# Six blocks of 512 columns in the first stage of a decoder trunk, four of them summed in SBUF from quarter pieces

## The chip, the core and the metric

The kernel runs on one core of a Trainium2 chip. The metric is the device time of one execution in microseconds (us), the median over executions. TensorE (PE in the profile) multiplies matrices, VectorE (DVE) and ScalarE (ACT) do elementwise work, SyncE (SP) issues nearly all DMAs, GpSimd (POOL) only eight small ones.

## The reference

A two-layer decoder trunk on 256 tokens of width 2048, all in float32. Layer 0 mixes with native sparse attention, layer 1 with stick-breaking attention; each is followed by a SwiGLU channel mixer. A vector c, one per sequence, gives each layer a shift, a scale and a gate (adaLN). What concerns the change is the start of layer 0:

```python
c_act = silu(c)
mod = c_act @ mod_w[0] + mod_b[0]                 # 2048 x 12288 weights
sh1, sc1, g1, sh2, sc2, g2 = split(mod, 6)
h = rms_norm(x, norm_g[0, 0]) * (1 + sc1) + sh1   # 256 x 2048
proj = h @ a_w_in                                 # 2048 x 5168
q, kc, vc, ks, vs, kw, vw, g = split(proj, ...)   # q: 2048 columns, six of 512, g: 48
q, kc, ks, kw = rope(...)                         # kc, vc: then compressed by an MLP (cmp_w1, cmp_w2)
o = gates[0]*attend(q, kc', vc') + gates[1]*attend(q, ks, vs) + gates[2]*attend(q, kw, vw)
x = x + g1 * rms_norm(o @ a_w_out, norm_g[0, 1])
```

## The kernel before, in words

Everything is read once from HBM, 657 MB. A weight comes in pieces of 512 rows by 512 columns, 1 MB each (`raw`). ACT rounds a piece to fp32r (`wh`), DVE takes the rest (`wl`), and TensorE multiplies three times for each 128 rows: `hh*wh`, `hh*wl`, `hl*wh`, where `hh` and `hl` are the same two parts of the activations (one page `hA` for each quarter of the 2048 rows). A piece is so 4 x 3 = 12 matmuls of 512 columns for each of the two token tiles t, 24 in all. A block of 512 output columns needs four such pieces, one for each quarter of the rows; its two accumulators (`acc`, one for each t) are two of the eight PSUM banks.

The shift and the scale of layer 0 must be known before the first `hA`. They are computed in quarters of 512 columns: eight loads of 1 MB (`modq`, four row quarters of two vectors), each used by four matmuls with a 32-column result (`qacc`); ACT copies the sum (`qrow`), TensorE transposes it (`pmq`), DVE adds it up (`mall`), and ACT and DVE make `hA` from it. The other vectors (`modw` loads, 16 for each vector) are multiplied and summed by DVE (`macc`, one instruction for each load); when a vector's sum is complete, four matmuls (`pmod`) add it up over the partitions (`mod_fin`).

The first stage before takes three blocks (kc, vc, ks) quarter by quarter: all three are held in six banks from quarter 0 to quarter 3. Then come kw, the first compression weights (`rawd`, which are not split), vs, the second ones, vw, the gates (`gacc`), four blocks of q, and under those the attention of 16 heads (`cs`, `sc`, `oT`), then the output projection (`wh,oA`) and the channel mixer.

The order on every engine is written out ahead by a planner (class `Emit`), which walks through the units of TensorE's work and gives each instruction a start and an end by a table of costs (`_cost`). It decides when a loaded piece is split, when a `macc` step is taken, and which work of the epilogues (generators, `spawn`) comes between the matmuls. On the chip each engine takes its instructions strictly in the order that the planner wrote. Buffers: 21 pages of 128 x 2048 (weights, `hA`, loads, sums), eight half-size `s2` buffers, eight banks. At most RAW_AHEAD = 7 loads are outstanding ahead of their splitting; SP issues them in the order of the list `order`, which is made at the end of the program. `when_free` and `get` keep MM_BANKS banks for accumulators.

Of the kernel before, what the change touches and what calls it, by code (L numbers as in the profile page):

```python
# [39 lines left out]
N_BANKS = 8  # L40
MM_BANKS = 3
RAW_AHEAD = 7
SPLIT_AHEAD = 2
# [3 lines left out]
LAGR = 1  # L47
K_LATE = 1
TAIL = 6
TAIL0 = 6  # L50
HEAD = 2
HEAD0 = 0
T1_LEAD = 2.0
# [83 lines left out]
class Emit:  # L137
# [4 lines left out]
    def __init__(self, nc):  # L142
# [16 lines left out]
        self.ahead = 0  # L159
        self.target = SPLIT_AHEAD  # L160
        self.reserve = SPLIT_AHEAD
        self.wait_pages = 0
# [64 lines left out]
    def when_free(self, tag):  # L227

        f = self.free[BANKS.get(tag, tag)]
        keep = max(0, MM_BANKS - self.mm) if tag == "x" else 0  # L230
        return f[0] if len(f) > keep else None

    def get(self, tag, name, *a, keep=0):
# [3 lines left out]
        while True:  # L237
            f = self.free[BANKS.get(tag, tag)]
            low = len(f) <= keep + (max(0, MM_BANKS - self.mm) if tag == "x" else 0)
# [166 lines left out]
def kernel(ctx: ExitStack, tc, consts, x, c, mod_w, mod_b, norm_g, ffn_w_in, ffn_w_out, a_w_in,  # L406
# [108 lines left out]
    def mac_load(vec, k):  # L515
# [6 lines left out]
        def mac(sl):  # L522
# [329 lines left out]

    def rope_T(acc, t, dst, tag="mm"):

# [8 lines left out]
        V.tensor_tensor(v1, av, cosT[:, t].unsqueeze(1).to_broadcast([P, 4, DH]), op=OP.mult)  # L863
        E.put(tag)
        V.tensor_tensor(t1, t1, t2, op=OP.add)
# [31 lines left out]

    def ep_k(acc, t, name, i, tag):
        dst = yield from get_kv(name)
        yield from rope_T(acc, t, dst[:, i], tag=tag)  # L900
        E.flag((name, i, t))
# [5 lines left out]

    def ep_v(acc, t, i):
        dst = yield from get_kv("v")
        copy(dst.rearrange("p s g n -> p s (g n)").rearrange("p s (t n) -> p s t n", t=2)[:, i, t], acc)  # L910
        E.put("mm")
        E.flag(("v", i, t))

    gates = {}
# [39 lines left out]

    def ep_q(acc, t, g):
        dst = yield from get_q("A", g)
        yield from rope_T(acc, t, dst)
        E.flag(("q", g, t))
# [301 lines left out]
    def emit_lag(us, lag):  # L1260
# [3 lines left out]
        while j < len(us):  # L1264
# [10 lines left out]
    col = {"q": 0, "kc": 2048, "vc": 2560, "ks": 3072, "vs": 3584, "kw": 4096, "vw": 4608, "g": 5120}  # L1275
    ko = [mm_units("kc", w0, col["kc"], 0, range(4), "hA", lambda a, t, nb: ep_k(a, t, "kvc", 0, "mm")),
          mm_units("vc", w0, col["vc"], 0, range(4), "hA", lambda a, t, nb: ep_vc(a, t)),
          mm_units("ks", w0, col["ks"], 0, range(4), "hA", lambda a, t, nb: ep_k(a, t, "ksw", 0, "mm"))]
    for kt in range(KT):
        for blk in ko:  # L1280
            units.extend(blk[kt])
    n_ko = len(units)
    emit_plain(mm_units("kw", w0, col["kw"], 0, range(4), "hA", lambda a, t, nb: ep_k(a, t, "ksw", 1, "mm")))
    for i in range(4):
        units.append(dict(kind="cmp", key=("w1", 0, i), s=0, i=i))
    emit_plain(mm_units("vs", w0, col["vs"], 0, range(4), "hA", lambda a, t, nb: ep_v(a, t, 0)))
    for i in range(4):
        units.append(dict(kind="cmp", key=("w1", 1, i), s=1, i=i))
    emit_plain(mm_units("vw", w0, col["vw"], 0, range(4), "hA", lambda a, t, nb: ep_v(a, t, 1)))
    units.append(dict(kind="gate", key=("wg",)))  # L1290
    for g in range(4):
        emit_plain(mm_units("q", w0, col["q"] + g * NB, g, range(4), "hA", lambda a, t, nb: ep_q(a, t, nb)))

# [260 lines left out]
```

## Time and profile before

| | us |
|---|---|
| median of three runs (2491.67 to 2493.23) | 2492.37 |
| profiled execution, time | 2491.2 |
| its span, first to last instruction | 2489.4 |
| PE busy | 2381.8 |
| DVE busy | 1584.3 |
| ACT busy | 1072.8 |

What lies outside the span is 1.8 us. The page gives PE as busy for 96% of the span and as 90% of the chain of work that ended last. Matmuls overlap, so a PE that is busy by the page isn't one at its peak: one matmul of 512 columns has a duration of 0.39 us, while the next one starts 0.23 us after it. An idle PE, or one at a lower granted clock, is what the rows below show.

### The profile page before, as it was taken

To read this page: it belongs to the slowest core of one execution; us is meant where nothing else is said; L and a number is where in the kernel's file an instruction comes from. 1 tells how busy PE (TensorE), PEld (TensorE's weight loads), DVE (VectorE), ACT (ScalarE), POOL (GpSimd) and SP (SyncE) were. 2 spreads that over 40 slices of the span, in tenths; PEclk is the share of its full clock that TensorE was granted. 3 is DMA by queue.
4 is the path that set the end of the run, shared out by engine and by line. 5 is a ranking of instruction groups with operands and counts; after the bars stand their busy time and mean duration, and the time that the engine had idled before them with its cause. 6 is when DMAs were issued, how large, how long until landed. Compare 5 with 4: busy or idle time off the path is not lost.

```text
span 2489.4 us, 26996 instructions
## 1 busy us (share of the span) xinstructions
PE 2381.8 (96%) x11086; PEld 1916.5 (77%) x11086; DVE 1584.3 (64%) x1275; ACT 1072.8 (43%) x1195; POOL 4.5 (0%) x12
## 2 busy tenths in 40 slices
PE   5789999998999999999998999999899999999998
PEld 2467777787888787878877887888788888888787
DVE  2357878968777666767767777775655544554554
ACT  3232355455333334333445455665533334434442
POOL 0000000000000000000000000000000000000000
PEclk9899999999999999999999999999999999999999
DMA  9979956767988779877757979776565646865642
GB/s 353 386 268 375 364 185 220 269 239 281 343 296 296 267 269 373 323 271 286 288 200 273 381 245 354 254 282 224 203 221 201 203 169 215 309 203 190 215 170 102
DMA packets 261532, 657.54 MB, mean 264 GB/s; under 512 B 12448, under 2 KB 21920, under 8 KB 236064
## 3 DMA queue, kind: packets, MB, share of 16 engines
q1 hardware_dynamic: 260704, 651.59, 72.9%
q0 software_dynamic: 704, 4.23, 0.4%
q8 instruction: 87, 1.43, 0.2%
q14 instruction: 37, 0.30, 0.0%
HBM read 653.64 MB, written 2.13 MB: 263 GB/s over the span
## 4 chain that ended last, share of the span: by engine, by line
PE 90%; DVE 4%; ACT 4%; issue 1%; DMA 0%; SPq 0%; DVEq 0%; ACTq 0%
PE acc L109 82%; DVE wl L109 1%; ACT wh L109 1%; PE z L109 1%; PE qacc L109 1%; PE sc L109 1%; PE oT L109 1%; DVE macc L109 1%; PE aT L109 1%; PE pmod L109 1%; ACT hf L109 1%; PE hid L109 1%; PE hT L109 1%; DMA modq<-in_mod_w_dram 0%; SPq L109 0%
## 5 line engine op out<-in xcount | busy, mean ns | idle before, releaser
L109 DVE TENSOR_TENSOR wl<-raw,wh 128x2048 fp32r<-128x2048 f32 x385 | 878.5, 2287 | 569.5 <-ACT wh L109 512.5
L109 ACT ACTIVATE wh<-raw 128x2048 fp32r<-128x2048 f32 x385 | 732.3, 1910 | 632.6 <-PE acc L109 452.0
L109 PE MATMUL acc<-wh,hhF 128*128 128x512 f32 x2816 | 882.2, 391 | 1.2 <-ACT hhF L109 1.1
L109 PEld LDWEIGHTS acc<-wh,hhF 128*128 128x128 f32 x2816 | 529.3, 188 | 115.6 <-issue 2.5
L109 PE MATMUL acc<-wl,hhF 128*128 128x512 f32 x1408 | 548.8, 390 | 1.1 <-DVE wl L109 1.1
L109 PE MATMUL acc<-wh,fa 128*128 128x512 f32 x1408 | 436.6, 390 | 0.0
L109 DVE SCALAR_TENSOR_TENSOR macc<-modw,cact,macc 128x2048 f32<-128x2048 f32 x180 | 422.3, 2346 | 11.4 <-DMA modw<-in_mod_w_dram 8.6
L109 PEld LDWEIGHTS acc<-wl,hhF 128*128 128x128 f32 x1408 | 264.8, 188 | 55.5 <-DVE wl L109 1.9
L109 PEld LDWEIGHTS acc<-wh,fa 128*128 128x128 f32 x1408 | 264.3, 188 | 55.4 <-issue 0.8
L109 PE MATMUL acc<-wl,fa 128*128 128x512 f32 x704 | 273.9, 389 | 0.0
L109 PE MATMUL acc<-wh,hA 128*128 128x512 f32 x640 | 226.0, 413 | 19.0 <-ACT wh L109 19.0
L109 PEld LDWEIGHTS acc<-wh,hA 128*128 128x128 f32 x640 | 123.8, 193 | 67.1 <-issue 22.3
L109 PE MATMUL acc<-wh,hhK 128*128 128x512 f32 x512 | 164.5, 398 | 3.0 <-ACT hhK L109 2.6
L109 PEld LDWEIGHTS acc<-wl,fa 128*128 128x128 f32 x704 | 132.2, 188 | 27.2
L109 PE MATMUL acc<-wl,hA 128*128 128x512 f32 x320 | 128.7, 402 | 8.7 <-DVE wl L109 8.7
L109 PEld LDWEIGHTS acc<-wh,hhK 128*128 128x128 f32 x512 | 97.3, 190 | 24.8 <-ACT hhK L109 2.8
L109 PE MATMUL acc<-wl,hhK 128*128 128x512 f32 x256 | 100.8, 394 | 3.2 <-DVE wl L109 3.2
L109 ACT ACTIVATE fa<-aT 128x512 fp32r<-128x512 f32 x43 | 25.6, 595 | 175.3 <-PE aT L109 160.5
L109 PE MATMUL acc<-wh,hhB 128*128 128x512 f32 x256 | 86.7, 404 | 1.8 <-ACT wh L109 1.8
L109 PE MATMUL acc<-wh,oA 128*128 128x512 f32 x256 | 83.0, 396 | 0.0
L109 PE MATMUL acc<-wh,oB 128*128 128x512 f32 x256 | 82.1, 394 | 0.0
L109 PEld LDWEIGHTS acc<-wl,hA 128*128 128x128 f32 x320 | 62.1, 194 | 21.3 <-DVE wl L109 11.2
(175 smaller groups left out, 1619.5 us busy)
## 6 DMA issues: line engine op xcount, KB each, us to landing
raw<-in_ffn_w_in_dram SPq DMA_DIRECT2D x176, 1024.0 KB, 5.5
modw<-in_mod_w_dram SPq DMA_DIRECT2D x160, 1024.0 KB, 7.1
raw<-in_ffn_w_out_dram SPq DMA_DIRECT2D x88, 1024.0 KB, 5.2
raw<-in_a_w_in_dram SPq DMA_DIRECT2D x40, 1024.0 KB, 10.1
modq<-in_mod_w_dram SPq DMA_DIRECT2D x32, 1024.0 KB, 14.3
modw<-in_kv_mod_w_dram SPq DMA_DIRECT2D x32, 1024.0 KB, 5.1
raw<-in_kv_w_dram SPq DMA_DIRECT2D x32, 1024.0 KB, 8.7
raw<-in_a_w_out_dram SPq DMA_DIRECT2D x16, 1024.0 KB, 5.7
```

Of the source, the lines that this page charges most:

```text
L109: return f(*a, **k)
```

## The change

1. The first stage takes six blocks in each quarter: kc and vc accumulate in four banks as before; ks, kw, vs and vw are computed in pieces of one quarter (`ep_piece`): each piece has a bank of its own for 12 matmuls. The first quarter is copied to a `part` page by ACT, the next ones are added to it by DVE, and at the last quarter rope works from `part` (ks, kw) or the sum is written to `v` (vs, vw).
2. In the first stage six banks are kept for accumulators (MM_START), afterwards three as before.
3. The list of loads: all eight `modq` of quarter 0, then the six weights of a quarter with the eight `modq` of the next quarter between them, and in the first three quarters one `modw` behind them. The first vector's four `modq` come before the second's.
4. After the first stage: the first block of q, the first compression weights, the gates, the second ones, and the other three blocks of q. Five keys (HEAD0) are passed before further `modw` are spread.
5. The planner's costs for matmuls, DMA and some DVE forms are others, and `mod_fin` starts 2.0 us later in the plan.

```diff
-K_LATE = 1
+MM_START = 6
+EARLY_Q = 0
-HEAD0 = 0
+HEAD0 = 5
+EXTRA_AT = (5,)
...
         if op == "transpose":
-            return 0.107
-        if out.shape[0] <= 64 and ins[1].dtype == F32 and n >= 256:
-            return n * 4 / 2400.0 * (0.25 if out.shape[0] <= 32 else 0.5)
-        return max(n * (4 if ins[1].dtype == F32 else 1) / 2400.0, 0.104)
+            return 0.109
+        if ins[1].dtype != F32:
+            return max(n / 2400.0 + 0.0133, 0.04)
+        if out.shape[0] <= 64 and n >= 256:
+            return n / 2400.0 + 0.09 if out.shape[0] <= 32 else n * 2 / 2400.0 + 0.02
+        return 2 * max(n * 2 / 2400.0 + 0.0133, 0.109)
...
     if eng == "DMA":
-        return n * 4 * P / 360e3 + 0.05
+        return n * 4 * P / 383e3
...
-    return 0.07 + n / (1920.0 if fast else 960.0)
+    ptr = 0.055 * (op in ("tensor_scalar", "scalar_tensor_tensor"))
+    return 0.075 + ptr + n / (1920.0 if fast else 960.0)
...
-        keep = max(0, MM_BANKS - self.mm) if tag == "x" else 0
+        keep = max(0, self.mm_banks - self.mm) if tag == "x" else 0
...
-                    E.spawn(mod_fin(vec))
+                    E.spawn(after(mod_fin(vec), E.fin + 2.0))
...
+    def ep_piece(acc, t, place, p, final):
+
+        if p:
+            yield from E.wait(("part", place, t, p - 1))
+        s = yield from part_of(place, t)
+        if p == KT - 1 and final[0] == "v":
+            yield from ep_v(acc, t, final[1], s, lambda: part_done(place))
+            return
+        if p == 0:
+            A.activation(s, acc, AF.Copy)
+        else:
+            V.tensor_tensor(s, acc, s, op=OP.add)
+        E.put("mm")
+        E.flag(("part", place, t, p))
+        if p == KT - 1:
+            yield
+            if final[0] == "q":
+                yield from ep_q(s, t, final[1], lambda: part_done(place))
+            else:
+                yield from ep_k(s, t, "ksw", final[1], lambda: part_done(place))
...
+    early = [("ks", 0, (0, 0), ("k", 0)), ("kw", 0, (0, 1), ("k", 1)), ("vs", 0, (1, 0), ("v", 0)),
+             ("vw", 0, (1, 1), ("v", 1))] + [("q", g, (2, g), ("q", g)) for g in range(EARLY_Q)]
     for kt in range(KT):
-        for blk in ko:
+        for blk in whole:
             units.extend(blk[kt])
+        for seg, nb, place, final in early:
+            emit_plain(mm_units(seg, w0, col[seg] + nb * NB, nb, [kt], "hA",
+                                lambda a, t, nb_, place=place, final=final, kt=kt: ep_piece(a, t, place, kt, final)))
     n_ko = len(units)
...
+    call(lambda: setattr(E, "mm_banks", MM_BANKS))
+    late = [mm_units("q", w0, col["q"] + g * NB, g, range(4), "hA", lambda a, t, nb: ep_q(a, t, nb))
+            for g in range(EARLY_Q, 4)]
+    emit_plain(late[0])
+    for s in range(2):
+        for i in range(4):
+            units.append(dict(kind="cmp", key=("w1", s, i), s=s, i=i))
+        if s == 0:
+            units.append(dict(kind="gate", key=("wg",)))
+    for blk in late[1:]:
+        emit_plain(blk)
...
     k0 = keys_of(0, n_ko)
+    qs = [[("modq", (0, i), q, kt) for i in (1, 0) for kt in range(KT)] for q in range(KT)]
+    order += qs[0]
+    m0 = mods_of([(0, 2), (0, 4), (0, 3)])
+    per = len(k0) // KT
     for q in range(KT):
-        order += [("modq", (0, i), q, kt) for i, kt in ((1, 0), (0, 2), (1, 1), (0, 3), (0, 0), (1, 2), (0, 1), (1, 3))]
-        order += k0[max(0, q * 3 - K_LATE):q * 3 + 3 - K_LATE]
-    order += k0[len(k0) - K_LATE:]
-    order += spread(keys_of(n_ko, n_l0), mods_of([(0, 2), (0, 4), (0, 3)]), TAIL0, HEAD0)
+        ws, ms = k0[q * per:(q + 1) * per], qs[q + 1] if q + 1 < KT else []
+        for i, w in enumerate(ws):
+            order.append(w)
+            order += ms[i * len(ms) // per:(i + 1) * len(ms) // per]
+            if q < KT - 1 and i in EXTRA_AT:
+                order.append(m0.pop(0))
+    order += spread(keys_of(n_ko, n_l0), m0, TAIL0, HEAD0)
```

TensorE executes the same number of instructions; DVE gets 19 more and ACT 10 more.

The order on TensorE at the end of a quarter, before (`hA_79` is the page of the second quarter of rows, and `wh_110` ends that quarter):

```order
L109 MATMUL acc_70_378<-wl_90_465,hA_79_434 128x512
L109 MATMUL acc_70_378<-wh_89_464,hA_79_434 128x512
L109 MATMUL qacc_95_499<-modq_91_468,cact_116 32x512 x4
L109 MATMUL pmq_103_583<-K_67,qrow_102_581 128x128 x4
L109 MATMUL qacc_93_483<-modq_94_488,cact_116 32x512 x4
L109 MATMUL pmq_106_598<-K_67,qrow_105_596 128x128 x4
L109 MATMUL acc_88_457<-wh_110_617,hA_79_434 128x512
L109 MATMUL acc_88_457<-wl_111_618,hA_79_434 128x512
L109 MATMUL acc_88_457<-wh_110_617,hA_79_434 128x512 x2
L109 MATMUL acc_88_457<-wl_111_618,hA_79_434 128x512
```

The last `modq` and both transposes stand behind all matmuls whose weights are split; TensorE goes on with `wh_110`, the quarter's last piece, which stands on ACT behind the next `hA`.

The same place in the change (`hA_52` is the page of quarter 0, `pmq_96` the last transposes of the next quarter's vectors):

```order
L111 MATMUL acc_93_499<-wh_81_432,hA_52_290 128x512
L111 MATMUL qacc_79_419<-modq_72_385,cact_116 32x512 x4
L111 MATMUL acc_93_499<-wh_81_432,hA_52_290 128x512
L111 MATMUL acc_93_499<-wl_82_433,hA_52_290 128x512
L111 MATMUL acc_93_499<-wh_81_432,hA_52_290 128x512
L111 MATMUL pmq_96_515<-K_67,qrow_95_513 128x128 x4
L111 MATMUL acc_93_499<-wh_81_432,hA_52_290 128x512
L111 MATMUL acc_93_499<-wl_82_433,hA_52_290 128x512
L111 MATMUL acc_93_499<-wh_81_432,hA_52_290 128x512 x2
```

Behind `pmq_96` stand 42 matmuls of quarter 0 and one `modq` until the first matmul with `hA_97`, the page of quarter 1.

DVE in the second quarter of the change (`part` are the sums, `wl` the split weights, `mall` and `hA` the next quarter's activations):

```order
L111 TENSOR_TENSOR wl_125_696<-raw_106_562,wh_124_695 128x2048
L111 TENSOR_TENSOR part_85_442<-acc_127_701,part_85_442 128x512
L111 TENSOR_TENSOR wl_131_735<-raw_113_603,wh_130_734 128x2048
L111 TENSOR_TENSOR part_85_442<-acc_128_714,part_85_442 128x512
L111 TENSOR_TENSOR part_85_442<-acc_133_740,part_85_442 128x512
L111 TENSOR_REDUCE mall_118<-pmq_138_779 128x4
L111 TENSOR_TENSOR mall_118<-mall_118,vecT_109 128x4
L111 TENSOR_SCALAR hf_140_790<-xnT_21_156,mall_118 128x256
L111 CAST hA_139_789<-hf_140_790 128x512
L111 TENSOR_TENSOR hA_139_789<-hf_140_790,hA_139_789 128x512
L111 TENSOR_TENSOR hA_139_789<-hf_141_795,hA_139_789 128x512
L111 TENSOR_TENSOR wl_143_801<-raw_115_637,wh_142_800 128x2048
```

The additions to `part` stand between the splits of the next weights, and `wl_143`, the quarter's last piece, stands behind the next quarter's `hA_139`.

TensorE at one of the partition sums (`pmod`) in layer 0's channel mixer, before and then in the change:

```order
L109 MATMUL acc_872_5448<-wl_864_5395,hhF0_630_3752 128x512
L109 MATMUL acc_872_5448<-wh_863_5394,hhF0_630_3752 128x512
L109 MATMUL pmod_874_5464<-macc_768_4676,K_67 32x512 x4
L109 MATMUL acc_869_5431<-wh_867_5427,hhF0_635_3778 128x512
L109 MATMUL acc_869_5431<-wl_868_5428,hhF0_635_3778 128x512
L109 MATMUL acc_869_5431<-wh_867_5427,hhF0_635_3778 128x512
```

```order
L111 MATMUL acc_898_5502<-wh_894_5483,hhF0_660_3824 128x512
L111 MATMUL acc_898_5502<-wl_895_5484,hhF0_660_3824 128x512
L111 MATMUL acc_898_5502<-wh_894_5483,hhF0_660_3824 128x512
L111 MATMUL pmod_903_5539<-macc_787_4666,K_67 32x512 x4
L111 MATMUL acc_898_5502<-wh_894_5483,hhF0_660_3824 128x512
L111 MATMUL acc_898_5502<-wl_895_5484,hhF0_660_3824 128x512
```

In the plan `pmod` may stand no earlier than 2.0 us after its sum's end, where it stood as soon as the sum was there; here it moves into a unit that has begun.

## Rows read from the trace of the kernel before

**Rows 1.** The page: busy time, share of the span and instructions of each engine.

```profile
PE 2381.8 (96%) x11086; PEld 1916.5 (77%) x11086; DVE 1584.3 (64%) x1275; ACT 1072.8 (43%) x1195; POOL 4.5 (0%) x12
```

**Rows 2.** Who waited for whom, TensorE, 39 to 152 us: total, times, longest.

```profile
PE acc L109 <- ACT wh L109: 19.0, 4, 4.8
...
PE pmq L109 <- ACT qrow L109: 4.3, 6, 0.7
```

**Rows 3.** TensorE in order of time at a quarter's end: start, duration, instruction, idle before.

```profile
105.41 1.06 PE L109 MATMUL qacc<-modq,cact 128*32 128x512 f32 x8
107.19 0.66 PE L109 MATMUL pmq<-K,qrow 128*128 128x128 f32 x4 [0.72 <-ACT qrow L109]
112.58 0.80 PE L109 MATMUL acc<-wh,hA 128*128 128x512 f32 x1 [4.74 <-ACT wh L109]
114.91 0.80 PE L109 MATMUL acc<-wl,hA 128*128 128x512 f32 x1 [1.53 <-DVE wl L109]
115.50 1.05 PE L109 MATMUL acc<-wh,hA 128*128 128x512 f32 x2
116.36 0.63 PE L109 MATMUL acc<-wl,hA 128*128 128x512 f32 x1
```

**Rows 4.** Windows of that end: length, busy by engine, clock, DMA share, GB/s.

```profile
107.85:112.58 4.73, 0.00 (x0) 0.00 (x0) 2.74 (x8) 4.06 (x6) 0.00 (x0) 0.92 1.05 388
112.58:120.74 8.16, 6.62 (x19) 4.67 (x19) 6.68 (x3) 3.55 (x2) 0.00 (x0) 0.63 1.05 387
83.47:107.85 24.38, 22.94 (x127) 11.75 (x126) 0.34 (x2) 1.19 (x2) 0.00 (x0) 1.00 1.04 386
```

**Rows 5.** TensorE in order of time within that quarter.

```profile
93.93 1.06 PE L109 MATMUL qacc<-modq,cact 128*32 128x512 f32 x8
94.93 0.50 PE L109 MATMUL acc<-wh,hA 128*128 128x512 f32 x1
95.26 0.39 PE L109 MATMUL acc<-wl,hA 128*128 128x512 f32 x1
95.49 0.62 PE L109 MATMUL acc<-wh,hA 128*128 128x512 f32 x2
95.96 0.40 PE L109 MATMUL acc<-wl,hA 128*128 128x512 f32 x1
```

**Rows 6.** Groups by line: busy, mean ns of one, idle before.

```profile
L109 DVE TENSOR_TENSOR wl<-raw,wh 128x2048 fp32r<-128x2048 f32 x385 | 878.5, 2287 | 569.5 <-ACT wh L109 512.5 <-PE acc L109 41.6 <-DMA raw<-in_ffn_w_in_dram 8.6
L109 ACT ACTIVATE wh<-raw 128x2048 fp32r<-128x2048 f32 x385 | 732.3, 1910 | 632.6 <-PE acc L109 452.0 <-DVE wl L109 87.2 <-DVE macc L109 38.1
...
L109 DVE SCALAR_TENSOR_TENSOR macc<-modw,cact,macc 128x2048 f32<-128x2048 f32 x180 | 422.3, 2346 | 11.4 <-DMA modw<-in_mod_w_dram 8.6 <-DMA modw<-in_kv_mod_w_dram 2.4
...
L109 DVE TENSOR_TENSOR yp<-acc,yp 128x512 f32<-128x512 f32 x16 | 11.0, 687 | 24.4 <-PE acc L109 24.4
...
L109 ACT ACTIVATE yp<-acc 128x512 f32<-128x512 f32 x16 | 9.4, 590 | 13.1 <-DVE wl L109 6.6 <-PE acc L109 6.5
...
L109 PE MATMUL hid<-rawd,xpe 128*64 128x256 f32 x128 | 14.7, 384 | 0.0
```

**Rows 7.** Windows of the stages behind the first one.

```profile
190.00:300.00 110.00, 102.94 (x554) 83.89 (x553) 81.10 (x56) 34.36 (x28) 0.00 (x0) 0.98 1.03 387
300.00:550.00 250.00, 242.54 (x1246) 189.01 (x1245) 202.44 (x329) 135.09 (x282) 1.16 (x2) 0.99 0.65 228
```

**Rows 8.** The same view, instructions on macc alone.

```profile
150.00:300.00 150.00, 1.93 (x8) 0.20 (x8) 51.73 (x23) 0.97 0.91 339
300.00:550.00 250.00, 2.13 (x16) 0.34 (x16) 57.58 (x25) 0.99 0.65 228
```

**Rows 9.** Who waited for whom, TensorE, the whole span.

```profile
PE pmod L109 <- DVE macc L109: 12.0, 7, 3.1
```

**Rows 10.** The same view, 152 to 560 us.

```profile
PE acc L109 <- DVE wl L109: 4.1, 2, 2.6
...
PE cs L109 <- DVE pc L109: 2.9, 1, 2.9
```

**Rows 11.** TensorE in order of time, the first weight piece.

```profile
44.03 0.80 PE L109 MATMUL acc<-wh,hA 128*128 128x512 f32 x1 [4.80 <-ACT wh L109]
```

More of the change, by code (lines that the diff above doesn't have):

```diff
@@ L160, in __init__ @@
         self.target = SPLIT_AHEAD
+        self.mm_banks = MM_START
         self.reserve = SPLIT_AHEAD
@@ L238, in get @@
             f = self.free[BANKS.get(tag, tag)]
-            low = len(f) <= keep + (max(0, MM_BANKS - self.mm) if tag == "x" else 0)
+            low = len(f) <= keep + (max(0, self.mm_banks - self.mm) if tag == "x" else 0)
             if not low and f[0] <= self.now + 0.2:
@@ L851, with put_mm, rope_T @@
     qT = {}
-    def rope_T(acc, t, dst, tag="mm"):
+    def put_mm():
+        E.put("mm")
+    def rope_T(acc, t, dst, done):
         av = acc.rearrange("p (h d) -> p h d", h=4)
@@ L863, in rope_T @@
         V.tensor_tensor(v1, av, cosT[:, t].unsqueeze(1).to_broadcast([P, 4, DH]), op=OP.mult)
-        E.put(tag)
+        done()
         V.tensor_tensor(t1, t1, t2, op=OP.add)
@@ L896, in plain_T, with ep_k @@
         yield from T_out(s, t, dst)
-    def ep_k(acc, t, name, i, tag):
+    def ep_k(acc, t, name, i, done=put_mm):
         dst = yield from get_kv(name)
-        yield from rope_T(acc, t, dst[:, i], tag=tag)
+        yield from rope_T(acc, t, dst[:, i], done)
         E.flag((name, i, t))
@@ L906, in ep_vc, with ep_v, part_of, part_done @@
         E.flag(("kvc", 1, t))
-    def ep_v(acc, t, i):
+    def ep_v(acc, t, i, part, done):
         dst = yield from get_kv("v")
-        copy(dst.rearrange("p s g n -> p s (g n)").rearrange("p s (t n) -> p s t n", t=2)[:, i, t], acc)
+        d = dst.rearrange("p s g n -> p s (g n)").rearrange("p s (t n) -> p s t n", t=2)[:, i, t]
+        V.tensor_tensor(d, acc, part, op=OP.add)
         E.put("mm")
+        done()
         E.flag(("v", i, t))
+    spage = {}
+    sleft = {}
+    def part_of(place, t):
+        pg, half = place
+        if pg not in spage:
+            spage[pg] = None
+            spage[pg] = yield from E.get("pg", "part")
+            sleft[pg] = 4
+        while spage[pg] is None:
+            yield False
+        return spage[pg][:, (half * 2 + t) * NB:(half * 2 + t + 1) * NB]
+    def part_done(place):
+        sleft[place[0]] -= 1
+        if sleft[place[0]] == 0:
+            E.put("pg")
+    def ep_piece(acc, t, place, p, final):
[9 more added lines that the diff above has]
+            V.tensor_tensor(s, acc, s, op=OP.add)
+        E.put("mm")
+        E.flag(("part", place, t, p))
[5 more added lines that the diff above has]
+                yield from ep_k(s, t, "ksw", final[1], lambda: part_done(place))
     gates = {}
@@ L953, in q_done, with ep_q @@
             E.put("pg")
-    def ep_q(acc, t, g):
+    def ep_q(acc, t, g, done=put_mm):
         dst = yield from get_q("A", g)
-        yield from rope_T(acc, t, dst)
+        yield from rope_T(acc, t, dst, done)
         E.flag(("q", g, t))
@@ L1275 @@
     col = {"q": 0, "kc": 2048, "vc": 2560, "ks": 3072, "vs": 3584, "kw": 4096, "vw": 4608, "g": 5120}
-    ko = [mm_units("kc", w0, col["kc"], 0, range(4), "hA", lambda a, t, nb: ep_k(a, t, "kvc", 0, "mm")),
-          mm_units("vc", w0, col["vc"], 0, range(4), "hA", lambda a, t, nb: ep_vc(a, t)),
-          mm_units("ks", w0, col["ks"], 0, range(4), "hA", lambda a, t, nb: ep_k(a, t, "ksw", 0, "mm"))]
+    whole = [mm_units("kc", w0, col["kc"], 0, range(4), "hA", lambda a, t, nb: ep_k(a, t, "kvc", 0)),
+             mm_units("vc", w0, col["vc"], 0, range(4), "hA", lambda a, t, nb: ep_vc(a, t))]
+    early = [("ks", 0, (0, 0), ("k", 0)), ("kw", 0, (0, 1), ("k", 1)), ("vs", 0, (1, 0), ("v", 0)),
+             ("vw", 0, (1, 1), ("v", 1))] + [("q", g, (2, g), ("q", g)) for g in range(EARLY_Q)]
     for kt in range(KT):
-        for blk in ko:
+        for blk in whole:
             units.extend(blk[kt])
+        for seg, nb, place, final in early:
+            emit_plain(mm_units(seg, w0, col[seg] + nb * NB, nb, [kt], "hA",
+                                lambda a, t, nb_, place=place, final=final, kt=kt: ep_piece(a, t, place, kt, final)))
     n_ko = len(units)
[L1283 to L1292, printed above, removed]
+    call(lambda: setattr(E, "mm_banks", MM_BANKS))
[9 more added lines that the diff above has]
+        emit_plain(blk)
     def out_units(seg, W, lhs, epi):
```

## The prediction

> **What bounds the kernel now.** I read the page first, then TensorE's waits, then the time order of the stretch that the change rewrites, then windows behind it. TensorE is busy for 2381.8 us of the 2489.4 us span [rows 1], and it executes the same instructions after the change; so the question is what becomes of the time in which it waits or runs at a lower clock. Its waits between 39 and 152 us are nearly all one pattern [rows 2]: four waits for the rounding of a weight (19.0 us in all) and six for the copy of a vector's sum (4.3 us). Rows 3 show one of them in order of time, the end of a quarter. The last four-matmul group of a vector starts at 105.41, its transposes at 107.19, and then nothing is left that TensorE could do: the next weight piece is rounded on ACT behind the making of the next activations, and its first product starts at 112.58, its second at 114.91 [rows 3]. Behind the pause the clock granted is 0.63 of full speed over 8.16 us [rows 4], which is a mixture of the two levels, 1.2 and 2.4 GHz: two matmuls take 0.86 us there (115.50 to 116.36) [rows 3], three take 0.70 us within the quarter (95.26 to 95.96) [rows 5], that is 0.43 against 0.233 us each. DMA is not what TensorE waits for: its share stays at 1.04 to 1.05 and it moves 386 to 388 GB/s through pause and work alike [rows 4], so that a load of 1 MB (1.0486 million bytes) takes 2.71 us, and the loads run ahead of their use.
>
> **The change part by part.** The sum is made against the profiled execution, 2491.2 us; the median of the runs is 1.2 us above it.
>
> *The ends of the quarters.* One end costs 4.73 us of idle time [rows 4], two waits of 0.72 us for the copies [rows 3], and a slow run-in: 8.16 us for 19 matmuls [rows 4] that at 0.233 us each would take 4.4, so 3.7 us, the wait of 1.53 us for the second product in it. Together 9.9 us. There are three such ends; the fourth wait, before the first quarter, stays, since its loads come first in both lists. After the change the last transposes of the next quarter's vectors stand in the middle of a quarter, with 42 matmuls and one vector group of this quarter behind them. A vector group takes 1.00 us (93.93 to 94.93) and delays the next matmul by another 0.1 (0.33 instead of 0.23 us to the one after) [rows 5]. So the cover is 42 x 0.233 + 1.1 = 10.9 us; from the start of the transposes to the second product of the next piece the chain takes 7.7 us (107.19 to 114.91) [rows 3]. The ends go: 3 x 9.9 = 29.7 us.
>
> Here a rule speaks against the change. Rows 4 show that with the quarters of rows outermost TensorE keeps its full clock for 24.38 us (1.00) as long as work is there, and loses it behind a pause of 4.73 us. The Trainium skill, "TensorE: Matmul & The Clock Gate", section "HAM oscillation — how this bites in real kernels", advises to take all K tiles of an output before the next wait, as a loop with the K tiles outermost went cold in each of them. The change keeps them outermost and makes each longer. By the rule the run-ins would stay and three times 2.2 us (3.7 without the 1.53) of the gain would be lost; by the row they go with the pauses, and I take that.
>
> *What the longer quarter is bound by.* Six pieces are 144 matmuls x 0.233 = 33.6 us, eight vector groups 8.8 us, two transposes of about 0.6 us [rows 3] 1.2 us: 43.6 us on TensorE. DMA brings 15 loads in that time, 40.6 us; TensorE stays the bound by 3.0 us a quarter. DVE has six splits of 2.287, eight additions and a macc step of 2.346 us [rows 6]: an addition to a sum in SBUF is the same instruction as yp<-acc,yp, 0.687 us, a first copy is ACT's yp<-acc, 0.590 us [rows 6]. That is 21.6 us of 43.6: the 20 additions to `part` (13.7 us) and eight copies (4.7 us) lie beside matmuls. What is queued behind them: at the second end the split wl_143 stands behind the making of hA_139, and TensorE reaches its first use after 28 matmuls and the transposes, 7.1 us, against 7.7 us of chain; at the third end a macc step and an addition also stand ahead of the next split, 10.7 us against 9.7 us of matmuls. A piece's bank must be empty when the next but one begins, 2.8 us (12 x 0.233) later; a drain that finds a split running takes up to 2.29 + 0.69 = 3.0 us. I take 3 us for all of this; the bounds are 0 and 16 (0.2 us for each of the 32 outputs that are summed in pieces, and one end's 9.9 us back).
>
> *Behind the first stage.* Before, four weight pieces lay between the two sets of compression loads. Now the eight loads, the gates' weights (0.4 MB) and nine modw follow each other, with the next block's first weight 18.4 loads in 50 us of DMA, while the compression matmuls are 14.7 us [rows 6] and the gates about 6. DMA must so be 30 us ahead at their start. It can be: the ten weights before them are 56 us of TensorE and 27 us of loads, but seven outstanding loads are 19 us only. In this stretch DMA was already at 1.03 with TensorE idle for 7.1 of 110 us [rows 7]. I take 4 us; the bounds are 0 and 15.
>
> *The attention.* By its start DVE has taken 23 macc steps before [rows 8] and 14 in the new order. Nine more steps, 21 us, fall into the 250 us of attention and output projection, where DVE was busy for 202.4 us [rows 7]: 81% becomes 89%. TensorE idled there for 7.5 us, 2.9 of it in one wait for DVE's softmax of the compressed scores [rows 10]. Each such instruction may find a macc step of 2.35 us ahead of it. The bounds are 0 and 21; I take 5 us.
>
> *The later partition sums.* TensorE waited 12.0 us in seven waits for DVE's macc before the sum over partitions, 3.1 us at most [rows 9]. Two microseconds later in the plan put other matmuls there, which shortens each wait by up to 2 us; DVE is no earlier for it, and some come back at the next split. I take 5 us saved, between 0 and 12. That the costs of the plan are nearer to rows (a matmul of 0.2267 us in it instead of 0.2133) I count at nothing: it changes no instruction's duration, and what it does to the order is in the terms above.
>
> The sum: 2491.2 - 29.7 + 3 + 4 + 5 - 5 = 2468.5; 2469 us for the median.
>
> **The rivals.** *DVE takes over.* The nine steps and the softmax stand on one engine. If TensorE waits for all 21 us, the sum is 2484.5 us. For it: 89% on average leaves little for the peaks. Against it: the steps are due only at the end of the projection, and at 81% only 7.5 us were lost.
>
> *The banks, slower than before.* Two banks change hands among 32 outputs (four blocks, two token tiles, four quarters). If a drain stands behind a split and a macc step, it takes 2.29 + 2.35 + 0.69 = 5.3 us where 2.8 are free, 2.5 us late, in half the outputs 40 us: 2508 us. It decides from 0.7 us an output (22.7 / 32). For it: DVE takes its list strictly in order, and additions and splits alternate in it. Against it: one macc step a quarter isn't one for each output, and DVE is half idle there.
>
> *The loads.* If page space lets DMA run no further ahead than seven loads, the compression stage costs its 15 us and the gain is the smaller by 11: 2479.5 us.
>
> *The clock.* If TensorE paused briefly at each change of bank and fell to the lower level now and then, a fifth of the stage's 576 matmuls at 0.43 instead of 0.233 us would cost 23 us: 2491 us, no change. In the rows the clock fell only behind a pause of 4.7 us [rows 4]. The Trainium skill states such a thing, on the same page under "A second HAM failure mode: psum-queue depth-cycling": a kernel that cycled through banks lost its clock in short pauses between groups. No run here has shown it yet.
>
> **How the numbers follow.** The forecast 0.72 (its own range 2455 to 2480), DVE 0.12, the loads 0.06, the banks 0.07, the clock 0.03. The lowest sum of the bounds is 2491.2 - 29.7 - 12 = 2449.5; upwards the range takes in DVE and the loads, not the banks: 2449 to 2487. A measurement of this kernel tells about 0.2% (5 us) from no change. The forecast, most of DVE's case and the loads are faster: 0.88; the clock and what is left of DVE's case the same: 0.04; the banks, and mishaps of several terms together, slower: 0.08.
>
> **What would show it.** In the profile after, TensorE's waits for `wh` before 152 us should be one of 4.8 us, not four, those for `qrow` nearly none, and the granted clock 1.00 from some 55 us to the stage's end. The 24 weight pieces of the first stage should end near 213 us: from 44 us on [rows 11] three quarters of 43.6, the last of 33.6, and a run-in of about 5. Waits for DVE's macc before `pmod` should fall to about 7 us. Wrong would be: pauses in each quarter that end with a DMA or with a `part` instruction (the loads, the banks), a clock below 1.00 without a pause, or the attention with more than 25 us of idle time on TensorE.

## The result, and the profile after

The changed kernel takes 2476.6 us (median of four runs, 2475.4 to 2478.4), the kernel before in the same comparison 2492.7: a ratio of 0.9937, 95% interval 0.9919 to 0.9954. It is 16 us faster; forecast were 22.7, 2469 us in a range of 2449 to 2487. The profiled execution has a span of 2473.5 us instead of 2489.4. The page's row of busy time, as in [rows 1]:

```profile
PE 2385.3 (96%) x11086; PEld 1911.0 (77%) x11086; DVE 1598.5 (65%) x1294; ACT 1078.9 (44%) x1205; POOL 4.5 (0%) x12
```

TensorE is idle for 88.2 us of the span (107.6 before) and executes the same 11086 instructions. TensorE's waits from 39 to 152 us, as in [rows 2]:

```profile
PE qacc L111 <- DMA modq<-in_mod_w_dram: 4.4, 1, 4.4
PE acc L111 <- DVE wl L111: 0.5, 1, 0.5
```

The waits for `wh` (19.0 us) and `qrow` (4.3 us) are gone; the only pause left lies before the first piece and now ends with a load. TensorE in order of time, at the place that answers to [rows 3]:

```profile
120.10 0.40 PE L111 MATMUL acc<-wh,hA 128*128 128x512 f32 x1
120.34 0.64 PE L111 MATMUL pmq<-K,qrow 128*128 128x128 f32 x4
120.73 0.47 PE L111 MATMUL acc<-wh,hA 128*128 128x512 f32 x1
...
127.86 0.50 PE L111 MATMUL acc<-wl,hA 128*128 128x512 f32 x1 [0.51 <-DVE wl L111]
```

The transposes of a vector stand between two matmuls of a piece, without a pause on either side. Two answers of the windows view, the first for the first stage, the second for what follows (columns as in [rows 4, 7]):

```profile
62.00:200.00 138.00, 137.49 (x678) 94.43 (x677) 81.05 (x85) 53.13 (x50) 0.00 (x0) 1.00 0.95 351
...
262.00:275.00 13.00, 7.57 (x50) 5.78 (x46) 9.69 (x5) 3.85 (x4) 0.00 (x0) 0.71 1.02 407
275.00:279.00 4.00, 4.00 (x14) 2.99 (x13) 3.56 (x3) 3.14 (x2) 0.00 (x0) 0.67 1.00 406
279.00:419.00 140.00, 131.71 (x693) 97.44 (x692) 117.69 (x222) 69.25 (x174) 0.00 (x0) 0.98 0.69 255
419.00:537.00 118.00, 112.91 (x556) 89.38 (x553) 99.66 (x112) 65.01 (x113) 1.17 (x2) 1.00 0.79 288
```

The full clock holds for 138 us of the first stage. Two places are worse than before: the end of the compression (262 to 275), where 5.4 us are lost in waits, with a clock of 0.71 and 0.67 in and behind it, and the attention (279 to 419), where TensorE idles for 8.3 us of 140; between the same two events of the kernel before it idled for 0.6 us of 128, with as many matmuls:

```profile
303.00:431.00 128.00, 127.42 (x693) 97.40 (x694) 105.64 (x218) 72.49 (x174) 0.00 (x0) 1.00 0.58 203
```

A smaller place is the end of the first stage, TensorE in order of time:

```profile
201.42 0.63 PE L111 MATMUL hT<-K,rp 128*128 128x128 f32 x4 [0.54 <-DVE rp L111]
203.33 0.66 PE L111 MATMUL hT<-K,rp 128*128 128x128 f32 x4 [1.28 <-DVE rp L111]
...
205.53 0.50 PE L111 MATMUL acc<-wl,hA 128*128 128x512 f32 x1 [1.31 <-DVE wl L111]
```

There the rope of the last pieces and the splits stand on DVE one behind the other, and behind the three waits, 3.1 us in all, a matmul takes 0.43 us until 209.2.

Where the time went, by three events of TensorE's order:

| from the span's start, us | before | after |
|---|---|---|
| first score product (`cs<-L,qT`) | 303.0 | 279.2 |
| first product of the channel mixer (`acc<-wh,hhF`) | 552.1 | 536.9 |
| last matmul | 2480.2 | 2464.3 |

At the first score product 684 weight matmuls are done instead of 672, 2.7 us more. So the first stage and the compression gained 26.5 us (23.8 + 2.7), the attention and the projection gave back 11.3 (257.7 - 249.1 + 2.7), the rest gained 0.7: 15.9 in all. A wait of 3.1 us of `pmod` for macc, the longest of [rows 9], stood at 265 us before and is not there any more; it is in the 26.5.

### The profile page after: what moved, and what is told of

Same layout as the page of the kernel before. It is cut to its first block, busy times and chain, and to the rows that moved or that the text cites. A ratio compares the mean times of both kernels' runs of the same rounds, so it can differ in the third digit from the quotient of the medians.

```text
span 2473.5 us, 27017 instructions
## 1 busy us (share of the span) xinstructions
PE 2385.3 (96%) x11086; PEld 1911.0 (77%) x11086; DVE 1598.5 (65%) x1294; ACT 1078.9 (44%) x1205; POOL 4.5 (0%) x12
## 4 chain that ended last, share of the span: by engine, by line
PE 77%; DVE 5%; DMA 4%; ACT 3%; issue 1%; SPq 0%; DVEq 0%; ACTq 0%
PE acc L111 72%; DMA modw<-in_mod_w_dram 2%; DVE wl L111 2%; DMA raw<-in_a_w_in_dram 2%; DVE macc L111 1%; PE z L111 1%; ACT wh L111 1%; PE aT L111 1%; PE pmod L111 1%; ACT hf L111 1%; PE sc L111 1%; DVE st L111 1%; ACT junk L111 0%; PE hid L111 0%; PE oT L111 0%
## 5 line engine op out<-in xcount | busy, mean ns | idle before, releaser
L111 DVE TENSOR_TENSOR wl<-raw,wh 128x2048 fp32r<-128x2048 f32 (+1 forms) x385 | 878.6, 2287 | 533.2 <-ACT wh L111 490.3
L111 ACT ACTIVATE wh<-raw 128x2048 fp32r<-128x2048 f32 (+1 forms) x385 | 733.1, 1910 | 669.6 <-PE acc L111 456.4
```

Of the source, the lines that this page charges most:

```text
L111: return f(*a, **k)
```

## The experiments

Each was timed against the kernel before; ratios have their 95% interval.

**The fifth part: costs of the plan, and mod_fin 2.0 us later**

*e1*, the changed kernel without the delay:

```diff
-                    E.spawn(after(mod_fin(vec), E.fin + 2.0))
+                    E.spawn(mod_fin(vec))
```

> The changed kernel with mod_fin started at once again, without the 2.0 us in the plan. Theory A (the term of the prediction): TensorE's waits for DVE's macc before pmod come back, about 12 us in seven waits instead of 4.3, and with them 5 us of time (between 0 and 12): about 2481 us. Theory B (the waits only change their place: in the profile after, 2.5 us of waits for sg and 0.7 for mrow stand where the waits for macc were): within 2 us of 2476.6.

Measured: 2513.3 us (2509.3 to 2521.0), 1.0091 (1.0076 to 1.0106). That is 37 us slower than the changed kernel and slower than the kernel before; neither theory had the size. TensorE's waits over the whole span:

```profile
PE pmod L111 <- DVE macc L111: 27.4, 10, 8.1
```

The longest, in order of time, first DVE, then TensorE:

```profile
1258.01 2.29 DVE L111 TENSOR_TENSOR wl<-raw,wh 128x2048 fp32r<-128x2048 f32 x1 [3.13 <-ACT wh L111]
1260.22 0.68 DVE L111 TENSOR_TENSOR yp<-acc,yp 128x512 f32<-128x512 f32 x1
1261.69 0.69 DVE L111 TENSOR_TENSOR yp<-yp,G 128x512 f32<-128x512 f32 x1 [0.79 <-ACT junk L111]
1262.30 2.35 DVE L111 SCALAR_TENSOR_TENSOR macc<-modw,cact,macc 128x2048 f32<-128x2048 f32 x1
```

```profile
1256.17 0.39 PE L111 MATMUL acc<-wh,fa 128*128 128x512 f32 x1
1264.70 1.93 PE L111 MATMUL pmod<-macc,K 128*32 128x512 f32 x8 [8.15 <-DVE macc L111]
```

Without the delay the plan puts `pmod` into TensorE's order while the last step of its vector is only entered in DVE's. On the chip that step stands behind a split that waits for ACT and two other instructions, and TensorE stands still for 8.15 us with matmuls queued behind `pmod`. Idle time grows by 25.2 us over the changed kernel, busy time, with the clock at a mean of 0.981 instead of 0.989, by 11.0.

*e5*, the kernel before with the new costs of `_cost` alone, and *e6*, the same with the 2.0 us as well:

```diff
-        return n * 4 * P / 360e3 + 0.05
+        return n * 4 * P / 383e3
...
+        return 2 * max(n * 2 / 2400.0 + 0.0133, 0.109)
...
-                    E.spawn(mod_fin(vec))                             # e6 alone
+                    E.spawn(after(mod_fin(vec), E.fin + 2.0))
```

> The kernel before with the new costs of the plan and nothing else of the change. Theory A (slack): with the old costs a matmul is planned at 0.2133 us and takes 0.2277, so on the chip TensorE comes later than planned and the other engines' results are there when it asks; with the nearer costs that slack is gone, as in the changed kernel without the 2.0 us, where the waits for macc before pmod were 27 us. Then these waits rise here too, from 12.0 to over 20 us, and the time by 12 to 25 us, to 2505 to 2518. Theory B (the prediction: the costs are worth nothing; the loss without the 2.0 us belongs to the new order of the first stage): 2488 to 2497.

> The kernel before with the new costs and the 2.0 us before mod_fin, the fifth part of the change alone; the first stage stays as it was. Theory A (slack): the 2.0 us give back what the costs took: the waits for macc before pmod are near the 4.3 us of the changed kernel and the time is within 5 us of before, 2487 to 2497; the first stage is then what brings the 16 us. Theory B (the fifth part brings a gain of its own): under 2484.

Measured: e5 2503.8 us (2499.2 to 2508.9), 1.0042 (1.0029 to 1.0056); e6 2481.3 us (2478.4 to 2483.5), 0.9952 (0.9940 to 0.9965). In e5 the waits of `pmod` are 27.0 us, as theory A had it, and the time lies a little under its 2505, because the first stage got faster: the first score product starts at 289.5 us, with 693 weight matmuls done. For e6 theory B holds: 11.7 us faster than before. The gain lies ahead of the attention: the first score product starts at 292.1 us with 690 weight matmuls done. That is 10.9 us earlier and 18 matmuls (4.1 us) further, 15.0 us gained, where the change gained 26.5. TensorE's waits of e6 from 39 to 165 us:

```profile
PE qacc L109 <- DMA modq<-in_mod_w_dram: 6.2, 1, 6.2
PE acc L109 <- DVE wl L109: 5.2, 3, 1.8
PE acc L109 <- ACT wh L109: 2.0, 3, 1.1
PE pmq L109 <- ACT qrow L109: 0.7, 1, 0.7
```

With three blocks and the old list of loads the pauses for `wh` are down to 1.1 us at most, from 4.8 [rows 2], by the costs alone (e5 has the same waits for `wh`). How this comes about is seen on ACT at the end of the second quarter, first before, then in e6:

```profile
108.49 1.58 ACT L109 ACTIVATE hf<-xnT,mall 128x256 f32<-128x256 f32 x3 [1.35 <-DVE mall L109]
110.64 5.49 ACT L109 ACTIVATE wh<-raw 128x2048 fp32r<-128x2048 f32 x3
```

```profile
101.41 3.70 ACT L109 ACTIVATE wh<-raw 128x2048 fp32r<-128x2048 f32 x2
106.15 1.09 ACT L109 ACTIVATE hf<-xnT,mall 128x256 f32<-128x256 f32 x2 [1.04 <-DVE mall L109]
```

Before, the rounding of the quarter's last weight stands behind the making of the next activations (`hf`, `hA`); in e6 it stands ahead of it. What is left are the waits for `wl`, up to 1.8 us, and slow matmuls behind them.

The two kinds of first stage and the three plans in one table:

| median, us | old costs | new costs | new costs and 2.0 us |
|---|---|---|---|
| three blocks | 2492.7 | 2503.8 | 2481.3 |
| six blocks | - | 2513.3 | 2476.6 |

The delay is worth 22.6 us in one row and 36.7 in the other. Without it the six blocks are 9.5 us slower than the three. With it they bring 4.6 us over the three; the intervals of 0.9952 and 0.9937 overlap. In the profiles, the six blocks gain 11.5 us more than e6 up to the first score product and give back 6.2 us more between there and the channel mixer (11.3 against 5.1).

*e10*, the kernel before with the load's cost alone (the first pair of lines of the diff above):

> The kernel before with one cost of the plan changed, that of a load: 2.74 us for 1 MB instead of 2.96; three blocks in the first stage, the old list of loads, the other costs and mod_fin as before. Theory A (the load's cost is what took the pauses out of the first stage where only the fifth part of the change was made): the four waits for wh, 19.0 us, fall under 8, the first score product starts 8 to 14 us earlier than at 303.0, and as the costs of matmuls stay, the waits of pmod for macc stay near 12 us: 2478 to 2485. Theory B (the matmuls' or DVE's costs did it): the pauses stay, 2488 to 2496.

Measured: 2524.6 us (2522.2 to 2525.4), 1.0130 (1.0115 to 1.0145), the slowest of all. Theory A fell. Waits of e10 from 39 to 165 us, then over the whole span:

```profile
PE acc L109 <- ACT wh L109: 14.2, 3, 4.7
...
PE pmod L109 <- DVE macc L109: 28.7, 9, 8.1
```

The pauses stay, and the waits of `pmod` go from 12.0 [rows 9] to 28.7 us by this one cost, with the matmuls' cost as it was. So the explanation in e5's theory A, slack in the matmuls' cost, isn't needed: the load's cost is enough. One reading is that a plan that thinks loads later than they are takes the steps later, when DVE on the chip is no longer behind; that was not tested by itself. Which cost takes the pauses out was not run alone. In the order that the plan writes, the load's cost alone, TensorE's alone and DVE's alone each leave the last rounding behind the next `hA`; the load's and TensorE's together put it ahead. The last transposes move little: they stand behind 48 of a middle quarter's 72 matmuls before and behind 45 in e5.

**The six blocks**

*e9*, the changed kernel with the old cost of a load:

```diff
-        return n * 4 * P / 383e3
+        return n * 4 * P / 360e3 + 0.05
```

> The changed kernel with one cost of the plan put back, that of a load: 2.96 us for 1 MB instead of 2.74 (the trace has 2.71). Theory A (cover: the six blocks give TensorE work enough at each quarter's end, whatever the plan thinks of the loads): no pause over 2 us at a quarter's end, the granted clock stays 1.00 from 60 to 200 us, and the first score product (cs) starts within 4 us of the 279.2 of the changed kernel; what the time then loses, it loses behind that. Theory B (the cost of a load does it: a plan that thinks the loads later than they are puts the next quarter's vector behind all of this quarter's weights): pauses with waits for wh come back at the quarters' ends and cs starts 8 us later or more.

Measured: 2481.2 us (2479.9 to 2485.3), 0.9958 (0.9946 to 0.9970). Theory A holds. Waits of e9 from 39 to 165 us, and the window of its first stage:

```profile
PE qacc L111 <- DMA modq<-in_mod_w_dram: 2.8, 1, 2.8
PE acc L111 <- DVE wl L111: 1.5, 1, 1.5
PE pmq L111 <- ACT qrow L111: 0.7, 1, 0.7
...
60.00:200.00 140.00, 138.61 (x686) 93.94 (x684) 77.69 (x81) 53.12 (x51) 0.00 (x0) 1.00 0.96 352
```

No wait for `wh`, a clock of 1.00, and the first score product at 279.6 us. The loss comes in the attention: the first product with `oA` starts at 432.7 us, in the changed kernel at 419.0. ACT in e9, at the end of the second quarter:

```profile
111.66 1.91 ACT L111 ACTIVATE wh<-raw 128x2048 fp32r<-128x2048 f32 x1 [0.56 <-DVE wl L111]
129.13 1.59 ACT L111 ACTIVATE hf<-xnT,mall 128x256 f32<-128x256 f32 x3 [1.27 <-DVE mall L111]
```

Behind a quarter's last transposes stand only 24 to 27 matmuls, about as many as before (24). But at this end their weight was rounded 15 us ahead of the next activations, where before it was rounded behind them.

**The attention and the compression**

*e2*, nine macc steps cut to 32 columns (the rest of those sums is left out), everything else in the same order:

```diff
+                c = slice(0, 32) if vec == (0, 4) and k < 10 else sl
-                V.scalar_tensor_tensor(macs[vec][:, sl], st["t"][:, sl], ...
+                V.scalar_tensor_tensor(macs[vec][:, c], st["t"][:, c], ...
```

> The changed kernel with nine macc steps (vector (0,4), k 1 to 9) that work on 32 of 2048 columns; the rest of those sums is left out. The loads and the order of all engines stay as they are; only DVE is relieved of 9 x 2.1 = 19 us between 305 us and about 380 us. Theory A: what the attention lost (11 us against before) is TensorE waiting behind DVE, whose list holds nine more macc steps there: the idle time between 340 and 420 us goes from 8.0 us to under 3 and the time falls by 6 to 11 us, to 2466 to 2470. Theory B: the loss comes from the new order of the heads and weights or from ACT and the banks: the time stays within 3 us of 2476.6.

Measured: 2474.4 us (2472.3 to 2479.5), 0.9933 (0.9920 to 0.9945). Theory A falls: 2.2 us under the changed kernel, with overlapping intervals. The window of e2's attention:

```profile
278.80:417.40 138.60, 131.23 (x692) 97.46 (x691) 99.72 (x222) 69.60 (x174) 0.00 (x0) 0.98 0.69 257
```

DVE is busy for 99.7 us instead of 117.7, and TensorE still idles for 7.4 instead of 8.3: the time that these steps take on DVE is not what it mainly waits for.

*e7*, the same nine steps taken out with their loads (that part of the vector is left out):

```diff
+    order = [k for k in order if not (k[0] == "mod" and k[1] == (0, 4) and 1 <= k[2] < 10)]
     for k in order:
```

> The changed kernel without the nine modw of vector (0,4), k 1 to 9: neither loaded nor summed, that part of the vector is left out. Theory A (pages and the queue: a modw that stands ahead of a weight in the list of loads makes the weight late, as at 396 to 407 us in the profile after, where three of them go ahead of the last weight of q): TensorE's waits for wh and wl in the attention, 5.1 us, and the slow clock behind them go, and 6 to 11 us come back: 2465 to 2470 us. Theory B (the heads' own chain of exponentials and sums, or the order of heads and weights): the waits for pT, pc and qT stay and the time is 2473 to 2478.

Measured: 2466.4 us (2463.0 to 2467.5), 0.9889 (0.9877 to 0.9902): theory A, 10 us faster than the changed kernel. The window of its attention:

```profile
277.70:398.80 121.10, 121.10 (x646) 90.38 (x645) 94.56 (x199) 64.46 (x158) 0.00 (x0) 1.00 0.64 223
```

TensorE idles for nothing and has its full clock. This window holds 646 of TensorE's instructions instead of 692, as some of the work moves behind its end; from the first score product to the channel mixer e7 takes 249.1 us, as long as before, and the changed kernel 257.7. So 8.6 of the 11.3 us come back. What e7 leaves out and e2 has are the nine loads; but without them the plan also orders the rest otherwise, so that the loads alone make the difference is not shown. How a load can do it is seen in the changed kernel: SyncE's longest wait from 375 to 397 us, its issues in order of time, and then ACT:

```profile
SPq L111 <- PE acc L111: 12.7, 1, 12.7
```

```profile
392.89 1.28 SPq L111 DMA_DIRECT2D modw<-in_mod_w_dram  x3
396.44 0.38 SPq L111 DMA_DIRECT2D raw<-in_a_w_in_dram  x1
```

```profile
406.86 1.91 ACT L111 ACTIVATE wh<-raw 128x2048 fp32r<-128x2048 f32 x1 [0.55 <-DMA raw<-in_a_w_in_dram]
```

SyncE waits 12.7 us before it issues the first of three `modw`, with the weight behind them in its list. The weight lands 10 us after its issue, and TensorE waits for both its parts:

```profile
408.82 0.50 PE L111 MATMUL acc<-wh,hA 128*128 128x512 f32 x1 [1.30 <-ACT wh L111]
411.14 0.79 PE L111 MATMUL acc<-wl,hA 128*128 128x512 f32 x1 [1.83 <-DVE wl L111]
```

*e3*, the gates behind both sets of compression weights (`if s == 1:`), and *e4*, two `modw` in a quarter (`EXTRA_AT = (2, 5)`):

> The changed kernel with the gates' unit behind the second compression weights instead of between the two. Theory A: the 5.4 us of idle time at 265 to 275 us and the slow run-in behind it (clock 0.71 and 0.81) are the chain of the compression's second layer (product, copy by DVE, transposes, activation with a table load by ACT) with no other work to cover it; the gates' 6 us cover it and the time falls by 5 to 8 us: 2469 to 2472. Theory B: the next block's first weight lands only at 268.2 us by the profile after, so TensorE would wait for it instead: 2474 to 2478, with a wait for wh or a DMA in place of those for hid.

> The changed kernel with two modw instead of one in each of the first three quarters (behind the third and the sixth weight). Theory A (DVE binds the attention, DMA the compression stage): three macc steps, 7.0 us of DVE, leave the attention, and three loads, 8.1 us of DMA, leave the compression stage, where the next weight lands earlier; a quarter has 16 loads, 43.4 us, against 43.6 us of TensorE: 3 to 7 us faster than the changed kernel, 2470 to 2474. Theory B: the quarter is at DMA's limit and its DVE list too full: pauses for a weight in the first stage cost more than comes back: 2477 to 2486.

Measured: e3 2479.9 us (2477.1 to 2484.4), 0.9948 (0.9935 to 0.9962); e4 2480.4 us (2478.6 to 2483.1), 0.9954 (0.9942 to 0.9967). Neither brings its gain. In e3 the waits for `hid` go (5.4 us between 262 and 275 after), and 2.0 us for the gates' own chain come; TensorE's waits of e3 from 240 to 280 us:

```profile
PE gt L111 <- ACT gs L111: 2.0, 1, 2.0
...
```

The score product starts 2.4 us earlier, and the stretch to the channel mixer, 261.3 us long instead of 257.7, takes more than that back. Most of e3's loss lies behind: in its profile, an execution of 2484.4 us, 7.9 us are lost from the first product of the channel mixer on; its cause stays open. In e4 the first stage and the compression wait 4.3 us for `wl` and 3.2 for `wh` instead of for `hid`.

**Versions meant to be faster**

*e8* puts one cost back:

```diff
-            return max(n / 2400.0 + 0.0133, 0.04)
+            return max(n / 2400.0, 0.04)
```

> The changed kernel with one cost of the plan put back: 0.2133 us for an fp32r matmul of 512 columns instead of 0.2267; the 2.0 us before mod_fin stay. Theory A (slack): TensorE runs 6% behind the plan again, and its waits for other engines (wl, pT, sg, macc, hid) fall everywhere, 5 to 10 us in all: 2467 to 2472. Theory B (the plan's exactness is worth something, or its order comes out at random): 2474 to 2486.

*e11* takes nine macc steps ahead of the compression weights, with fewer loads ahead:

```diff
-RAW_AHEAD = 7
+RAW_AHEAD = 6
-HEAD0 = 5
-EXTRA_AT = (5,)
+HEAD0 = 11
+EXTRA_AT = (2, 5)
...
-                    E.spawn(after(mod_fin(vec), E.fin + 2.0))
+                    E.spawn(after(mod_fin(vec), E.fin + 4.0))
...
-    order += spread(keys_of(n_ko, n_l0), m0, TAIL0, HEAD0)
+    kq = keys_of(n_ko, n_l0)
+    for _ in range(3):
+        order += [kq.pop(0), m0.pop(0)]
+    order += spread(kq, m0, TAIL0, HEAD0)
```

> A version meant to be faster than both: the changed kernel with two modw in each of the first three quarters and one behind each of the first three weights of q (nine macc steps before the compression weights, where DMA stood idle for lack of pages), no other modw until the second block of q, six loads ahead instead of seven, and 4.0 us before mod_fin. If the loads that stand ahead of the weights bind the attention, its 8.6 us come back in part: 2466 to 2472. If the first stage is at DMA's limit or DVE's list is too full in the second half of the attention, where 39 macc steps are left: 2475 to 2482.

*e12* is e11 up to the channel mixer and has e8's settings from there (MM_MORE is the 0.0133, FIN the 4.0 of e11):

```diff
     n_l0 = len(units)
+    call(lambda: globals().update(RAW_AHEAD=7, MM_MORE=0.0, FIN=2.0))
```

> A version meant to be faster than both: up to the first channel mixer the order of the ninth experiment's successor e11 (nine modw before the compression weights, six loads ahead, 4.0 us before mod_fin), from there on the settings of e8 (a matmul planned at 0.2133 us, seven loads ahead, 2.0 us). By the profiles, e11 reached the first product of the channel mixer at 525.7 us (the changed kernel at 536.9) and lost 6.6 and 6.7 us in the two stages behind it; e8 took 1917.1 us from that product to its last matmul (the changed kernel 1927.4). Theory A (the stages add up): 525.7 + 1917.1 and about 11 us behind the last matmul's start make 2454 us, 2452 to 2462. Theory B (what e11 lost behind the attention comes from the later macc steps and loads that it leaves to be done there, not from its settings): 2464 to 2476.

Measured: e8 2477.4 us (2475.9 to 2479.4), 0.9937 (0.9925 to 0.9949); e11 2477.1 us (2472.9 to 2484.4), 0.9941 (0.9928 to 0.9953); e12 2453.7 us (2447.8 to 2455.7), 0.9838 (0.9823 to 0.9853). e8 comes out as its theory B has it, e11 as its second case. For both the result is the changed kernel's, out of two halves: e8 loses 12 us by the channel mixer's start and gains 10 behind it; e11 starts it 11 us earlier and loses 13 in the two stages behind, where TensorE's waits for `sg` are 12.9 us. e12 has both good halves, as its theory A had it. Its row of busy time, and two events in order of time:

```profile
PE 2377.4 (97%) x11086; PEld 1911.4 (78%) x11086; DVE 1597.1 (65%) x1293; ACT 1078.9 (44%) x1206; POOL 4.5 (0%) x12
```

```profile
276.37 0.29 PE L111 MATMUL cs<-L,qT 128*128 128x15 f32 x2
...
522.23 0.39 PE L111 MATMUL acc<-wh,hhF 128*128 128x512 f32 x1
```

The score product starts at 276.4 us with 36 more weight matmuls done than in the changed kernel, the channel mixer 14.7 us earlier, and the time is 23 us under the changed kernel's. Which of e11's five edits is needed was not taken apart.

## Why the prediction was right, and where it was not

*The ends of the quarters* (-29.7). The pauses and the run-ins at the lower clock are gone, and one pause is left before the first piece. The quarters end at 90.4, 134.6, 176.8 and 218.6 us: the middle two take 44.2 and 42.2 us, forecast 43.6; the last one takes 41.8, not 33.6, as the transposes after rope and the waits at 201 to 206 us with the run-in at the lower clock behind them lie in it, so that the pieces end at 218.6 instead of 213. In the changed kernel the cover works as the step had it: 42 to 63 matmuls of the quarter stand behind its last transposes. But the count of matmuls isn't what decides: in e9 24 to 27 stand there, about as many as before, and there is still no pause, because the last weight is rounded ahead of the next activations. Whether that order comes of the six blocks or of the new list of loads was not run apart. What the prediction did not see is that six blocks are not the only way: in e6 the costs alone put the rounding ahead, and with three blocks 15.0 of the 26.5 us are gained.

The rule that speaks against the change, in the Trainium skill, "TensorE: Matmul & The Clock Gate", section "HAM oscillation — how this bites in real kernels", read as one on the order of the loops, would have left the run-ins: the trace disagrees, with a granted clock of 1.00 over 138 us and the quarters outermost. As the reason that section of the Trainium skill gives a wait for a load in each K tile, behind which the clock falls. With that the trace agrees: the clock fell in and behind pauses, as at 201 to 209 and 262 to 279 us.

*The longer quarter and the compression* (+3, +4). Without the 3.1 us of the `pmod` wait the two stages gained 23.4 us of the 29.7: by difference 6.3 were lost, 7 forecast. The 0.51 us at 127.86 are the wait for a split that the step worked out at the second end; no wait for a bank is seen up to 152 us. The loads do fall behind ahead of the compression, as the step had it: the window from 185 to 235 us, and SyncE's waits from 190 to 235:

```profile
185.00:235.00 50.00, 46.56 (x209) 37.51 (x208) 39.25 (x40) 17.86 (x15) 0.00 (x0) 0.97 0.51 176
```

```profile
SPq L111 <- DVE wl L111: 45.9, 6, 15.2
```

DMA moves 176 GB/s there, 388 from 100 to 150 us and 390 from 240 to 262, because SyncE waits for splits to free pages. That this is what costs the time at the compression's end is not shown: TensorE's two waits there (5.4 us) are for `hid`, the compression's own chain, with no other work in the order to cover it; the next weight's rounding starts only at 268.2 us, when it has landed.

*The attention* (+5): 11.3 us, within the bounds of 0 and 21 but twice the value taken, and this is the term that was mis-sized, by a wrong mechanism. The step named DVE's macc steps. They did move as forecast (34 instructions on `macc` behind the first score product, 25 before [rows 8]):

```profile
40.00:279.00 239.00, 31.79 (x14) 0.96 0.92 337
279.00:537.00 258.00, 77.63 (x34) 0.99 0.73 270
```

But by e2 19 us of them on DVE cost about 2 us, not clear of the noise, and by e7 they cost 10 with their loads (and with the order that the plan makes of them).

*The later partition sums* (-5): 3.1 us in the compression and 0.7 behind the attention. The waits of `pmod` fell as forecast; over the whole span, with the waits that grew instead, it is now:

```profile
PE aT L111 <- DVE sg L111: 4.5, 5, 1.9
PE pmod L111 <- DVE macc L111: 4.3, 1, 4.3
```

From the channel mixer on the waits of `pmod` are 4.1 us less than before and those of `aT` for `sg` 3.4 more: some came back at another place, as the step allowed.

*The costs of the plan* (0): this step failed. It counted the costs at nothing, as they change no instruction's duration and what they do to the order was to lie in the other terms; no other term has it. The net number stood because two large errors cancel, which is luck. Alone, the costs lose 10.9 us (e5), though they take most of the quarters' pauses away, and the 2.0 us then bring 22.6 (e6). The prediction bounded the delay's worth by 12.0 us, the waits of the kernel before [rows 9]; with the new costs 27 us of such waits stood at risk, and in the changed kernel the delay holds 37 us (e1). So 11.7 of the 16 us come without the six blocks (e6).

*The rivals.* DVE taking over: half its size came, but little of it by DVE (e2). The banks and the clock: not seen; the wait of 0.51 us left the clock at 1.00. The loads: right in kind as far as e7 shows it, but the price fell on the attention.

## What to carry to other kernels

Where an order is written out by a plan, a change of the plan's costs moves every engine's instructions and can't be counted at nothing: one cost alone gave +32 us here (e10). Costs nearer to the chip do not by themselves give a better order: with them the waits of `pmod` went from 12.0 to 27.0 us (e5). An instruction that can be stalled by another engine's in-order list may need slack put in on purpose (e1, e6). When a stage gets shorter, look at which loads now stand ahead of the next stage's weights before looking at how busy the engines are (e2, e7). And before making a stage larger to cover a pause, look at what stands ahead of the awaited instruction on its own engine: here it was the order of the rounding and the next activations on ACT (e6, e9).

## What was not expected of the hardware

Taking 18 us of work off DVE in a stretch in which it was busy for 84% (117.7 of 140 us) changed TensorE's idle time there by under 1 us, while one macc step of 2.35 us at a bad place in DVE's list, behind a split that waited for ACT, kept TensorE still for 8.15 us.
